# A fused decoder layer on one core: 52 weight blocks multiplied as one 512-column and one 256-column matmul per k-tile, with memory slots of 16 KB

## The chip, the core and the metric

The kernel runs on one core of one Trainium2 chip. The metric is the device time of one execution in microseconds (us). Its engines each run their own instructions in order: TensorE (PE in the profile, its weight loads PEld), VectorE (DVE), ScalarE (ACT), GpSimd (POOL) and SyncE (SP), which here only issues DMAs.

## What is computed

One decoder layer for 256 tokens of 1024 features, in float32: a first layer norm; a token mixer whose two branches (a matrix-memory LSTM of 4 heads, and a gated delta rule with 16 value heads) read one wide input projection; a cross attention into 256 memory tokens; and 32 experts, of which each token takes four. Cut to what matters:

```python
h = layer_norm(x, ln_in_g, ln_in_b)
proj = h @ w_in                                   # q,k,v,o of the LSTM; q,k,v,z of the delta rule; gates
y_ml  = rms(mlstm(q, k, v)) * sigmoid(mo) @ w_branch_ml
y_gdn = rms(delta_rule(conv(q, k, v))) * silu(gz) @ w_branch_gdn
mix = (sigmoid(gate_ml) * y_ml + sigmoid(gate_gdn) * y_gdn) @ w_mix_out
h = layer_norm(ALPHA * h + mix, ...)
h = layer_norm(ALPHA * h + attention(h @ wq, mem @ wk, mem @ wv) @ wo, ...)
out = layer_norm(ALPHA * h + experts(h, top4(softmax(h @ w_router))), ...)
```

All dense products (before the experts) are made to nearly full float32 precision out of a narrower multiply: a number a is held as a high part and a remainder, a = ah + al, and a product is wh·xh + wh·xl + wl·xh.

## The kernel before

**Dense part.** There are 76 blocks of [1024 × 256] weights. `run_blocks` takes them in a fixed order: the keys of the memory (xk, 4 blocks), the convolution's q, k and v (16), the LSTM's q/k (mqk, 4) and v (mv, 4), its gates (gm) and outputs (mo), the product with w_branch_ml (yml, 4), the gates gg (4) and gz (8), the product with w_branch_gdn (br, 8 blocks in pairs that sum into one output), mix (4), then xv (4), xq (4) and wo (4).

A block goes through four steps. SP loads it as two DMAs of 512 KB into one of two `w_raw` buffers (L125); ACT makes the high part in two pieces (L136), DVE the remainder (L137), into four `w_sp` buffers; PE multiplies each half (128 output columns, or 128 tokens where the block "moves", `tm`) over eight k-tiles, with three matmuls of 256 columns per k-tile (L159 to L161, or L154 to L156 for `tm`), 48 in a block. After the first half of the next block, the block's `evac` function reads the result, both halves in one bank of 512 columns of PSUM. `run_blocks` writes all this in one order for every engine; the split of the next block stands ahead of the half that runs.

**Side work.** Generators in `sides` are stepped once after each half: the inverse of the delta rule's triangular matrices (`gen_inv`, L637 and L639, on DVE, beside mqk and mv), the LSTM itself (L839 to L911), and the scan over chunks (L717 to L800, beside gm, mo, yml). No scheduler reorders any of it: what stands first on an engine runs first.

**PSUM** has eight banks: three for blocks (tag `pp`) and five for everything else (tag `pt`).

**Expert part.** 384 tiles of 1 MB stream through a ring of 21 buffers (`load_expert_tile`, L1120 for w_gu, L1124 for w_dn). Seven have a pool of their own (ew1), six lie in the 8 KB slots of `act1` that held dense activations before (ew2), the others in `w_raw`, `w_sp` and the space of a later pool. For each expert eight tiles feed L1636 (64 token slots as weights, 512 moving columns) and four feed L1678. SP issues a load when its buffer is released; a load that waits holds all that follow on SP.

Of the kernel before, what the change touches and what calls it, by code (L numbers as in the profile page):

```python
# [58 lines left out]
class Block:  # L59
    """One [1024, 256] block of weights: its product with 256 columns, and what follows it."""  # L60

    def __init__(self, w2d, r0, c0, x, tm=False, first=True, last=True, evac=None, before=None, after=None):
        self.w2d, self.r0, self.c0, self.x, self.tm = w2d, r0, c0, x, tm
        self.first, self.last, self.evac, self.before, self.after = first, last, evac, before, after
        self.ps, self.half_evac = None, None


@with_exitstack
def tile_layer(ctx: ExitStack, tc: tile.TileContext, A, out, stop=None):
# [14 lines left out]
    act1 = rctx.enter_context(tc.tile_pool(name="act1", bufs=6, side="right"))  # L84
# [3 lines left out]
    act2 = lctx.enter_context(tc.tile_pool(name="act2", bufs=9))  # L88
# [11 lines left out]
    def a2(shape, dt, name):  # L100
        return act2.tile(shape, dt, name=name, tag="a2")

# [13 lines left out]
    def load(b, by_cols=False):  # L116
        b.raw = wpool.tile([128, KT, 256], F32, name="w_raw", tag="w_raw", bufs=2)
        b.hi, b.lo = [], []
# [9 lines left out]
    def split_part(b, c):  # L128
        """the high part (float32r) and what is left: by rows where the block moves, else by columns"""
# [8 lines left out]
        b.hi.append(hi)  # L138
        b.lo.append(lo)

    def half(b, c, ks=None):
        xh, xl = b.x
        if b.ps is None:
            if b.last and not b.half_evac:
# [5 lines left out]
        for k in ks or range(KT):  # L150
            st, sp = b.first and k == 0, b.last and k == KT - 1
            if b.tm:
                wh, wl = b.hi[k // 4][:, k % 4], b.lo[k // 4][:, k % 4]
                nc.tensor.matmul(o, xh[:, k, cs], wh, start=st, stop=False, skip_group_check=True)  # L154
                nc.tensor.matmul(o, xh[:, k, cs], wl, start=False, stop=False, skip_group_check=True)  # L155
                nc.tensor.matmul(o, xl[:, k, cs], wh, start=False, stop=sp, skip_group_check=True)  # L156
            else:
                wh, wl = b.hi[c][:, k], b.lo[c][:, k]
                nc.tensor.matmul(o, wh, xh[:, k], start=st, stop=False, skip_group_check=True)  # L159
                nc.tensor.matmul(o, wh, xl[:, k], start=False, stop=False, skip_group_check=True)  # L160
                nc.tensor.matmul(o, wl, xh[:, k], start=False, stop=sp, skip_group_check=True)  # L161
# [1569 lines left out]
```

## Time and profile before

| | us |
|---|---|
| median of 3 runs | 1552.58 (1550.48 to 1554.14) |
| the profiled execution's own span | 1545.5 |
| PE busy in it | 1449.1 (94%) |
| DVE busy | 572.2 (37%) |
| ACT busy | 396.4 (26%) |
| dense part, to the restart of the weight stream | about 0 to 600 |
| experts | about 600 to 1545 |

The span lies 7.1 us under the median of the runs. Where a later row gives a DMA rate, it is of all the core's traffic in that stretch; a busy share is read stage by stage, since the dense part and the expert part have different limits.

### The profile page before, as it was taken

The page shows a single profiled execution, that of the slowest core. Times are in us where ns is not written, and L with a number is a line of the kernel's source. Part 1 is how long each engine was busy: PE and PEld are TensorE (multiplying, and loading weights), DVE is VectorE, ACT ScalarE, POOL GpSimd, SP SyncE. Part 2 cuts the span into 40 slices and gives each one's busy share as a digit, 9 for nine tenths or more (in the row PEclk, how much of TensorE's full clock was granted, in tenths as well). Part 3 has the DMA queues.
Part 4 walks back from the last instruction along what each step waited for, and adds up shares of the span by engine and source line. Part 5 has one row for each costly group of instructions (what it writes and reads, how often), then busy time and mean ns, then how long its engine had stood idle before and what let it go on. Part 6 is the DMA issues. An engine that isn't in the chain of part 4 may idle for free.

```text
span 1545.5 us, 22348 instructions
## 1 busy us (share of the span) xinstructions
PE 1449.1 (94%) x9411; PEld 871.8 (56%) x9411; DVE 572.2 (37%) x1030; ACT 396.4 (26%) x630; POOL 49.2 (3%) x85
## 2 busy tenths in 40 slices
PE   8899999999999999999999999999999899899894
PEld 7889999999999996333333333333333323323331
DVE  6788875766657564102112111111111111102102
ACT  5766646335534542101101101101001001101101
POOL 3000210000020000000000000000000000000000
PEclk9999999999999999999999999999999999999998
DMA  8444662244676988999999999999999999999995
GB/s 279 137 137 137 192 204 84 83 137 142 197 241 221 336 298 340 410 413 416 417 417 415 416 417 416 414 417 418 415 415 417 417 415 417 416 417 415 416 417 209
DMA packets 158040, 499.85 MB, mean 323 GB/s; under 512 B 9848, under 2 KB 88752, under 8 KB 124400
## 3 DMA queue, kind: packets, MB, share of 16 engines
q1 hardware_dynamic: 154704, 486.57, 80.8%
q0 software_dynamic: 3232, 11.80, 2.3%
q8 instruction: 76, 1.25, 0.3%
q14 instruction: 28, 0.23, 0.0%
HBM read 492.83 MB, written 5.51 MB: 322 GB/s over the span
## 4 chain that ended last, share of the span: by engine, by line
PE 67%; DMA 20%; DVE 7%; ACT 3%; issue 1%; SPq 0%; DVEq 0%; ACTq 0%
PE ps_y L1678 12%; DMA ew<-in_w_gu_dram 10%; PE ps_g L1636 9%; PE ps_u L1636 9%; DMA ew<-in_w_dn_dram 8%; PE ps_proj L159 6%; PE ps_proj L161 6%; PE ps_proj L160 6%; PE ps_xg L1391 4%; PE ps_proj L156 2%; PE ps_proj L154 2%; PE ps_proj L155 2%; PE ps_g L1359 2%; DVE w_sp L137 1%; DMA w_raw<-in_w_branch_gdn_dram 1%
## 5 line engine op out<-in xcount | busy, mean ns | idle before, releaser
L1636 PE MATMUL ps_g<-ew,xg 128*64 128x512 f32 x1024 | 266.7, 599 | 17.4 <-DMA ew<-in_w_gu_dram 17.3
L1495 DVE TENSOR_SCALAR sw_g<-ps_g 128x512 f32<-128x512 f32 x32 | 22.1, 692 | 668.5 <-PE ps_g L1636 668.5
L1636 PE MATMUL ps_u<-ew,xg 128*64 128x512 f32 x1024 | 263.2, 592 | 0.0
L1678 PE MATMUL ps_y<-ew,aT 128*64 128x512 f32 x1024 | 226.8, 595 | 9.2 <-ACT aT L1668 8.6
L137 DVE TENSOR_TENSOR w_sp<-w_raw,w_sp 128x1024 fp32r<-128x1024 f32 x152 | 183.9, 1222 | 97.5 <-ACT w_sp L136 96.8
L159 PE MATMUL ps_proj<-hT_hi,w_sp 128*128 128x256 f32 x640 | 186.1, 291 | 0.0
L160 PE MATMUL ps_proj<-hT_lo,w_sp 128*128 128x256 f32 x640 | 181.6, 284 | 0.0
L161 PE MATMUL ps_proj<-hT_hi,w_sp 128*128 128x256 f32 x640 | 181.5, 284 | 0.0
L136 ACT CAST w_sp<-w_raw 128x1024 fp32r<-128x1024 f32 x152 | 157.3, 1046 | 63.2 <-PE ps_proj L156 18.8
L1636 PEld LDWEIGHTS ps_g<-ew,xg 128*64 128x64 f32 x1024 | 67.1, 136 | 180.6 <-issue 119.4
L1636 PEld LDWEIGHTS ps_u<-ew,xg 128*64 128x64 f32 x1024 | 73.6, 137 | 146.2 <-issue 146.2
L1678 PEld LDWEIGHTS ps_y<-ew,aT 128*64 128x64 f32 x1024 | 70.7, 137 | 144.7 <-issue 126.2
L1497 ACT ACTIVATE sw_s<-sw_g 128x512 f32<-128x512 f32 x32 | 20.1, 629 | 464.2 <-DVE sw_g L1495 464.2
L159 PEld LDWEIGHTS ps_proj<-hT_hi,w_sp 128*128 128x128 f32 x640 | 123.0, 192 | 4.2 <-issue 2.8
L160 PEld LDWEIGHTS ps_proj<-hT_lo,w_sp 128*128 128x128 f32 x640 | 123.2, 192 | 0.0
L161 PEld LDWEIGHTS ps_proj<-hT_hi,w_sp 128*128 128x128 f32 x640 | 123.0, 192 | 0.0
L1681 ACT COPY y<-ps_y 128x512 f32<-128x512 f32 x32 | 18.7, 585 | 231.5 <-PE ps_y L1678 231.5
L1391 PEld LDWEIGHTS ps_xg<-oh,hres 128*128 128x128 f32 x512 | 58.5, 192 | 24.2 <-issue 23.2
L1391 PE MATMUL ps_xg<-oh,hres 128*128 128x128 f32 x512 | 61.5, 278 | 10.5 <-DVE oh L1382 10.4
L1508 PE MATMUL pacc<-y,ct 64*128 64x512 f32 x256 | 63.9, 616 | 0.7 <-ACT y L1681 0.7
L248 ACT ACTIVATE xg<-ps_xg,gbc 128x128 f32<-128x128 f32 x64 | 29.3, 457 | 97.6 <-DVE xg L250 97.6
L250 DVE TENSOR_SCALAR xg<-ps_xg,gbc 128x128 f32<-128x128 f32 x64 | 26.2, 410 | 57.6 <-PE ps_xg L1391 38.3
(443 smaller groups left out, 1853.8 us busy)
## 6 DMA issues: line engine op xcount, KB each, us to landing
ew<-in_w_gu_dram SPq DMA_DIRECT2D x256, 1024.0 KB, 19.9
ew<-in_w_dn_dram SPq DMA_DIRECT2D x127, 1024.0 KB, 20.1
w_raw<-in_w_in_dram SPq DMA_DIRECT2D x88, 512.0 KB, 4.5
w_raw<-in_w_branch_gdn_dram SPq DMA_DIRECT2D x16, 512.0 KB, 4.8
w_raw<-in_xa_wk_dram SPq DMA_DIRECT2D x8, 512.0 KB, 6.9
w_raw<-in_w_branch_ml_dram SPq DMA_DIRECT2D x8, 512.0 KB, 4.1
w_raw<-in_w_mix_out_dram SPq DMA_DIRECT2D x8, 512.0 KB, 4.7
w_raw<-in_xa_wv_dram SPq DMA_DIRECT2D x8, 512.0 KB, 4.5
```

The source lines that it names most:

```text
L136: nc.scalar.copy(hi, raw)
L137: nc.vector.tensor_sub(lo, raw, hi)
L154: nc.tensor.matmul(o, xh[:, k, cs], wh, start=st, stop=False, skip_group_check=True)
L155: nc.tensor.matmul(o, xh[:, k, cs], wl, start=False, stop=False, skip_group_check=True)
L156: nc.tensor.matmul(o, xl[:, k, cs], wh, start=False, stop=sp, skip_group_check=True)
L159: nc.tensor.matmul(o, wh, xh[:, k], start=st, stop=False, skip_group_check=True)
L160: nc.tensor.matmul(o, wh, xl[:, k], start=False, stop=False, skip_group_check=True)
L161: nc.tensor.matmul(o, wl, xh[:, k], start=False, stop=sp, skip_group_check=True)
L1391: nc.tensor.matmul(ps[k // 4][:, k % 4], z[:, t, k * 128:(k + 1) * 128], oh[:, t].rearrange("p e s -> p (e s)"), start=t == 0 and k % 4 == ...
L1508: nc.tensor.matmul(pacc[t][n], ct[q, t * 128:(t + 1) * 128], y[q], start=False, stop=e == NE - 1, skip_group_check=True)
L1636: nc.tensor.matmul(w[n * 64:n * 64 + 64], xg[:, k, ei], wt[e, k][:, c0 + n * 512:c0 + (n + 1) * 512], start=False, stop=k == KT - 1)
L1678: nc.tensor.matmul(py[n * 64:n * 64 + 64], aT[:, k % 4, k // 4], wd[:, n * 512:(n + 1) * 512], start=k == 0, stop=k == KT - 1)
```

## The change

**Wide blocks.** A block marked `wide` makes, per k-tile, one matmul of 512 columns (the high weights against the high and the low columns side by side) and one of 256 (the low weights against the high columns, into the right half of the same bank). The two halves of a bank are then added by `summed`: ACT copies the right 256 columns into SBUF, DVE adds the left ones. The words given with the change say 47 of 76 blocks; in the code 52 are marked: xk, mqk, mv, gm, mo, yml, gz, gg, br, xv and xq. That is 832 matmuls of 512 columns and 832 of 256 in place of 2496 of 256, and 48 outputs with 96 copies and 96 additions. The 24 blocks of the convolution, mix and wo stay.

The results of xk, mv and xv are put by `summed` where they are needed, and their 12 copies of 512 columns (L383, L821, L1188) go. In br, the gate product (L958) takes 512 columns at once, where it took two of 256.

**PSUM.** A wide block needs two banks, so `pp` has four and `pt` four.

**Memory.** High and low parts must lie in one tile, so slots are 16 KB: `act1` has 3 instead of 6 of 8 KB, `act2` 4 and one of 8 KB instead of 9. Two expert tiles of 1 MB then share one `act1` slot, which is released as a whole.

```diff
-        return psum.tile([128, 512], F32, name=name, tag="pp", bufs=3)
+        return psum.tile([128, 512], F32, name=name, tag="pp", bufs=4)
...
-        return psum.tile([128, 512], F32, name=name, tag="pt", bufs=5)
+        return psum.tile([128, 512], F32, name=name, tag="pt", bufs=4)
...
+    def pair(alloc, name):
+        return alloc([128, 2, KT, S], F32R, name)
...
         if b.ps is None:
-            if b.last and not b.half_evac:
+            if b.wide:
+                b.ps = [ps_proj("ps_proj0"), ps_proj("ps_proj1")]
+            elif b.last and not b.half_evac:
...
+                w = b.sp[c][:, :, k]
+                one, two, rest = w[:, 0], xp[:, :, k], (w[:, 1], xp[:, 0, k])
+            if b.wide:
+                nc.tensor.matmul(o, one, two, start=st, stop=False, skip_group_check=True)
+                nc.tensor.matmul(o[:, 256:], *rest, start=False, stop=sp, skip_group_check=True)
+            else:
+                nc.tensor.matmul(o, one, two[:, 0], start=st, stop=False, skip_group_check=True)
+                nc.tensor.matmul(o, one, two[:, 1], start=False, stop=False, skip_group_check=True)
+                nc.tensor.matmul(o, *rest, start=False, stop=sp, skip_group_check=True)
+
+    def summed(b, c):
+        if b.sum is None:
+            b.sum = b.dest() if b.dest else t2([128, 2, 256], "pj_sum")
+        p = b.ps[c]
+        nc.scalar.copy(b.sum[:, c], p[:, 256:])
+        nc.vector.tensor_add(b.sum[:, c], b.sum[:, c], p[:, :256])
...
                 half(b, c)
+                if c == 0 and prev is not None and prev.wide and prev.last:
+                    summed(prev, 1)
+                if c == 1 and b.wide and b.last:
+                    summed(b, 0)
                 step_sides()
                 if c == 0 and prev is not None and prev.last and prev.evac:
-                    spawn(prev.evac(prev.ps))
+                    spawn(prev.evac(prev.sum if prev.wide else prev.ps))
...
         elif r < R1 + 6:
-            w = a1([128, 2 * D], F32, "ew2")
+            if (r - R1) % 2 == 0:
+                W["two"] = a1([128, 2, 2 * D], F32, "ew2")
+            w = W["two"][:, (r - R1) % 2]
```

Two places show where the new instructions stand. The first is DVE in the stretch of mv, where L137 makes remainders of weights and L637 and L639 are the inverse (`inv`). Before:

```order
L137 TENSOR_TENSOR w_sp<-w_raw,w_sp 128x1024 x2
L637 TENSOR_TENSOR inv_1881<-inv_1880 128x11x21
L639 TENSOR_TENSOR inv_1880<-inv_1880,inv_1881 128x11x21
L637 TENSOR_TENSOR inv_1881<-inv_1880 128x10x22
L639 TENSOR_TENSOR inv_1880<-inv_1880,inv_1881 128x10x22
L637 TENSOR_TENSOR inv_1881<-inv_1880 128x9x23
L639 TENSOR_TENSOR inv_1880<-inv_1880,inv_1881 128x9x23
L637 TENSOR_TENSOR inv_1881<-inv_1880 128x8x24
L639 TENSOR_TENSOR inv_1880<-inv_1880,inv_1881 128x8x24
L137 TENSOR_TENSOR w_sp<-w_raw,w_sp 128x1024 x2
```

The same place after the change (L147 is the remainder, L669 and L671 the inverse, L184 the addition in `summed`, `mqkv` the tile that holds the LSTM's values):

```order
L147 TENSOR_TENSOR w_sp<-w_raw,w_sp 128x1024 x2
L184 TENSOR_TENSOR mqkv<-mqkv,ps_proj_2215 128x256
L669 TENSOR_TENSOR inv<-inv 128x11x21
L671 TENSOR_TENSOR inv<-inv 128x11x21
L669 TENSOR_TENSOR inv<-inv 128x10x22
L671 TENSOR_TENSOR inv<-inv 128x10x22
L184 TENSOR_TENSOR mqkv<-mqkv,ps_proj_2270 128x256
L669 TENSOR_TENSOR inv<-inv 128x9x23
L671 TENSOR_TENSOR inv<-inv 128x9x23
L669 TENSOR_TENSOR inv<-inv 128x8x24
L671 TENSOR_TENSOR inv<-inv 128x8x24
L147 TENSOR_TENSOR w_sp<-w_raw,w_sp 128x1024 x2
```

Each block now has two additions between the same remainders and the same eight instructions of the inverse; nothing leaves DVE there.

The second place is ACT in br, where L136 makes high parts of weights and L960 the high part of the merged branches (`mT`). Before:

```order
L136 CAST w_sp<-w_raw 128x1024 x5
L960 CAST mT_hi<-gg 128x512
L136 CAST w_sp<-w_raw 128x1024 x4
L960 CAST mT_hi<-gg 128x512
L136 CAST w_sp<-w_raw 128x1024 x4
```

And after (L146 is the high part of weights, L183 the copy in `summed`, L985 the high part of `mT`):

```order
L146 CAST w_sp<-w_raw 128x1024 x4
L183 COPY pj_sum<-ps_proj_4437 128x256
L146 CAST w_sp<-w_raw 128x1024
L183 COPY pj_sum<-ps_proj_4438 128x256
L985 CAST mT<-hm_gate 128x512
L146 CAST w_sp<-w_raw 128x1024 x3
L183 COPY pj_sum<-ps_proj_4524 128x256
L146 CAST w_sp<-w_raw 128x1024
L183 COPY pj_sum<-ps_proj_4525 128x256
```

Of the four casts of weights between two casts of `mT`, one now stands between two copies that wait for PE.

## Rows read from the trace of the kernel before

**Rows 1.** The page: busy time of each engine, its share of the span, its instructions.

```profile
PE 1449.1 (94%) x9411; PEld 871.8 (56%) x9411; DVE 572.2 (37%) x1030; ACT 396.4 (26%) x630; POOL 49.2 (3%) x85
```

**Rows 2.** Windows: stretch, its length, busy time of each engine, granted clock, DMA share, GB/s.

```profile
core 0: us, PE busy (x) PEld busy (x) DVE busy (x) ACT busy (x) POOL busy (x), PEclk, DMA share, GB/s
176.00:216.00 40.00, 40.00 (x336) 40.00 (x335) 37.61 (x76) 20.43 (x30) 0.00 (x0) 1.00 0.58 185
216.00:352.00 136.00, 135.30 (x1469) 123.96 (x1467) 87.17 (x133) 58.59 (x94) 8.43 (x13) 1.00 0.36 113
352.00:428.00 76.00, 75.40 (x632) 75.43 (x633) 50.52 (x55) 43.21 (x56) 2.05 (x4) 1.00 0.58 184
428.00:476.00 48.00, 46.34 (x383) 45.13 (x381) 27.28 (x33) 18.31 (x21) 6.77 (x15) 1.00 0.67 214
496.00:560.00 64.00, 63.93 (x492) 62.16 (x492) 38.95 (x52) 33.91 (x55) 1.62 (x3) 1.00 0.91 328
660.00:1520.00 860.00, 798.17 (x3946) 291.96 (x3942) 135.38 (x292) 77.02 (x145) 0.00 (x0) 1.00 1.02 416
```

**Rows 3.** Timeline of PE: start, duration, line, tiles, weights, moving columns.

```profile
239.88 0.28 PE L159 MATMUL ps_proj<-hT_hi,w_sp 128*128 128x256 f32 x1
240.00 0.28 PE L160 MATMUL ps_proj<-hT_lo,w_sp 128*128 128x256 f32 x1
```

**Rows 4.** Timeline of PE: small matmuls, eight in the first row.

```profile
66.50 1.06 PE L479 MATMUL ps_gtot<-r,stack 16*128 16x16 f32 x8
67.42 0.20 PE L483 MATMUL ps_gtot<-ident,row_tmp 4*128 4x4 f32 x1
```

**Rows 5.** Timeline of PE among the experts: three rows of four lie between.

```profile
892.22 1.03 PE L1636 MATMUL ps_g<-ew,xg 128*64 128x512 f32 x4
...
895.65 0.60 PE L1636 MATMUL ps_g<-ew,xg 128*64 128x512 f32 x2
```

**Rows 6.** Groups by line and form: busy time, mean ns, idle before.

```profile
L958 DVE TENSOR_TENSOR gg<-gg,ps_proj 128x256 f32<-128x256 f32 x8 | 3.1, 416 | 0.4 <-PE ps_proj L161 0.4
L862 ACT ACTIVATE hm<-ps_mn,ml_v 128x256 f32<-128x256 f32 x8 | 3.4, 471 | 1.8 <-DVE ml_v L860 1.8
L383 ACT COPY kT_sp<-ps_proj 128x512 f32<-128x512 f32 x4 | 2.3, 580 | 0.0
```

**Rows 7.** Timelines of DVE and of PE beside mv.

```profile
206.94 0.36 DVE L639 TENSOR_TENSOR inv<-inv,inv 128x192 f32<-128x192 f32 x1
207.22 2.35 DVE L137 TENSOR_TENSOR w_sp<-w_raw,w_sp 128x1024 fp32r<-128x1024 f32 x2
210.74 0.28 PE L155 MATMUL ps_proj<-w_sp,hT_hi 128*128 128x256 f32 x1
```

**Rows 8.** Timelines of DVE and PE in the scan.

```profile
282.90 0.69 DVE L721 TENSOR_TENSOR vP<-vP,sc_t 128x512 f32<-128x512 f32 x1
283.98 1.09 PE L729 MATMUL ps_vn<-vP,x_t 64*64 64x128 f32 x16
```

**Rows 9.** Br: ACT's casts as a group, then timelines of ACT and PE.

```profile
L136 ACT CAST w_sp<-w_raw 128x1024 fp32r<-128x1024 f32 x17 | 17.0, 1047 | 18.1 <-DMA w_raw<-in_w_branch_gdn_dram 17.3 <-PE ps_proj L161 0.9
425.40 0.60 ACT L931 ACTIVATE gate_s<-ps_proj 128x512 f32<-128x512 f32 x1 [3.71 <-PE ps_proj L161]
475.95 0.39 PE L156 MATMUL ps_proj<-w_sp,mT_lo 128*128 128x256 f32 x1 [0.23 <-DVE mT_lo L961]
```

**Rows 10.** Waits of PE in the first 70 us: total, times, longest.

```profile
PE ps_gcol L456 <- DVE stack L447: 3.0, 1, 3.0
```

**Rows 11.** SP's issues in the first expert; second and last row: median us to landing.

```profile
613.28 4.12 SPq L1120 DMA_DIRECT2D ew<-in_w_gu_dram  x2
ew<-in_w_gu_dram SPq DMA_DIRECT2D x1, 1024.0 KB, 10.5
622.17 2.04 SPq L1120 DMA_DIRECT2D ew<-in_w_gu_dram  x2
w_raw<-in_w_in_dram SPq DMA_DIRECT2D x88, 512.0 KB, 4.5
```

More of the change, by code (lines that the diff above doesn't have):

```diff
@@ L59, with __init__ @@
 class Block:
-    def __init__(self, w2d, r0, c0, x, tm=False, first=True, last=True, evac=None, before=None, after=None):
+    def __init__(self, w2d, r0, c0, x, tm=False, first=True, last=True, evac=None, before=None, after=None, wide=False,
+                 dest=None):
         self.w2d, self.r0, self.c0, self.x, self.tm = w2d, r0, c0, x, tm
@@ L65, in __init__ @@
         self.ps, self.half_evac = None, None
+        self.wide, self.dest, self.sum = wide, dest, None
 @with_exitstack
@@ L152, in half @@
             if b.tm:
[L153 to L156, printed above, removed]
-            else:
[L158 to L161, printed above, removed]
+                w = b.sp[k // 4][:, :, k % 4]
+                one, two, rest = xp[:, 0, k, cs], w, (xp[:, 1, k, cs], w[:, 0])
+            else:
+                w = b.sp[c][:, :, k]
[13 more added lines that the diff above has]
+        nc.vector.tensor_add(b.sum[:, c], b.sum[:, c], p[:, :256])
     def step_sides():
@@ L215, in run_blocks @@
             prev = b
+        if prev is not None and prev.wide and prev.last:
+            summed(prev, 1)
         if prev is not None and prev.evac:
-            spawn(prev.evac(prev.ps))
+            spawn(prev.evac(prev.sum if prev.wide else prev.ps))
     def evac_now(gen):
@@ L376, in gen_ln_in @@
             yield
-        for i, _ in enumerate(transpose_split(hres, hT_hi, hT_lo, gbc)):
+        for i, _ in enumerate(transpose_split(hres, hT, gbc)):
             if i % LK == LK - 1:
@@ L684, in f @@
             if not vP:
-                for i in range(2):
-                    vP.append(a2([128, 4, NCH, 128], F32, f"vP{i}"))
+                vP_ = a2([128, 2, 4, NCH, 128], F32, "vP")
+                vP.extend(vP_[:, i] for i in range(2))
             y = conv_taps(ps, 16 + 2 * u)
@@ L791, in gen_scan @@
         nc.vector.reciprocal(t, t)
-        oT = C["oT"] = [a2([128, KT, S], F32, f"oT{g}") for g in range(2)]
+        oT_ = a2([128, 2, KT, S], F32, "oT")
+        oT = C["oT"] = [oT_[:, g] for g in range(2)]
         for g in range(2):
@@ L991, in ev_norm @@
         return f
-    xh = (hT_hi, hT_lo)
+    xh = hT
     wbm, wbg = A["w_branch_ml"][0], A["w_branch_gdn"][0]
-    seq = [Block(A["xa_wk"][0], 0, u * 256, (memT_hi, memT_lo), evac=ev_xk(u)) for u in range(4)]
+    seq = [Block(A["xa_wk"][0], 0, u * 256, memT, evac=ev_xk(u), wide=True,
+                 dest=lambda u=u: kT_sp[:, 2 * u:2 * u + 2]) for u in range(4)]
     conv = []
@@ L1150, in affine2, with vk @@
         affine_col(dst, src, gbc[:, 16 + k:17 + k], gbc[:, 24 + k:25 + k], on_act)
+    def vk():
+        if "vk" not in XA:
+            XA["vk"] = a1([128, 2, 2 * D], F32, "xvk")
+        return XA["vk"]
     def gen_ln1():
```

192 lines of the change are left out of this document (92 added, 100 removed).

## The prediction, made before the changed kernel was run

> **What bounds the kernel now.** The first view is the page's list of busy engines [rows 1]: PE 94% of the span, and no other engine above 56%. That share is a mean over two regimes, so the second view is the windows [rows 2]. From 660 to 1520 us the DMA share is 1.02 at 416 GB/s: there the weight stream sets the time, and fewer PE instructions buy nothing. In the dense windows the DMA share is 0.36 to 0.67 up to 476 us, and PE is busy 40.00 of 40.00, 135.30 of 136, 75.40 of 76, 46.34 of 48: PE sets the time, except that DVE is nearly as full in the first of them (37.61 of 40) and that PE has holes in the last. The stream restarts from an empty queue at about 600 us, so what the dense part gains or loses moves the end by as much. The granted clock is 1.00, its higher level, in all these windows.
>
> **Price of a k-step.** In the window of 40.00 us PE made 336 matmuls of 256 columns: 119.0 ns each [rows 2], as the timeline shows one by one [rows 3]; a k-step of three costs 357 ns. Is this the columns or the loading of 128 columns of weights? Eight small matmuls with 128 weight columns but only 16 moving columns go from 66.50 to 67.42, 115 ns each [rows 4]: weights alone take nearly the whole pace. A matmul of 512 columns is seen among the experts: 16 from 892.22 to 895.65, 214.4 ns each [rows 5], with 64 weight columns. In a wide block the 512 columns should cover the loading, and the 256 columns after them stay at 119: 214.4 + 119.0 = 333.4 ns, 23.7 saved. Bounds: if the small one shrank to half of 214.4, the saving is 357 − 321.6 = 35 ns; if the 119.0 − 107.2 = 11.8 ns above the columns' share were a fixed cost of each matmul, one such is saved, 11.8 ns. I take 23.7, since the small matmuls point at the weights. A block has 16 k-steps, 0.38 us; 52 blocks 19.7 us, between 9.8 and 29.
>
> The Trainium skill, "TensorE: Matmul & The Clock Gate", section "Back-to-back issue gap", puts an isolated matmul at N/2.4 + 2.5 ns, 109 ns for 256 columns and 216 for 512; three would be 328 and the wide step 325, and the change would save 2 us in all. The trace disagrees on the first figure (119.0) and agrees on the second (214.4). Section "LDWEIGHTS" of that page puts the load of 128 columns at 107 ns by their number, near the 115 here; it lies on the side of the reading that I chose.
>
> **What is added.** Each of 48 outputs costs two copies on ACT and two additions on DVE. The nearest rows are a DVE product of 128x256 from PSUM, 416 ns, and an ACT instruction of 128x256 from PSUM, 471 ns; each copy of 580 ns that goes was one of 12 [rows 6]. So DVE gets 96 × 0.416 = 40 us, ACT 96 × 0.471 − 12 × 0.58 = 38 us. They cost nothing where these engines have room and PE does not wait behind them. Stretch by stage:
>
> *Front (xk, 4 blocks, −1.5 at best).* PE later waits 3.0 us for DVE's rows [rows 10]; what PE gains before runs into that wait, and additions in the same queue push it. I take +0.3, ends −1.5 and +1.0.
>
> *mqk, mv (8 blocks, −3.0 at best).* DVE runs here without a gap: the inverse's instruction of 206.94 ends where the remainders of 207.22 begin. Their first is needed at 210.74, and was done 2.35/2 after 207.22, at 208.4: 2.3 us of slack [rows 7]. The 16 additions are 6.7 us; the window's idle time takes 2.4 of them, that slack 2.3, and 2.0 would be left. But the inverse's instructions get shorter at its end, and the first gm block has more slack. I take 0: all of the 3.0 is lost; ends −1.5 and +4.3 (6.7 − 2.4).
>
> *gm, mo, yml (12 blocks, −4.5 at best).* DVE is busy 87.2 of 136 us and gets 10 more. But the scan runs through DVE: L721 ends at 283.59 and its matmuls start at 283.98 [rows 8], a margin of 0.39, less than one addition. I charge four such places, 4 × 0.42 = 1.7, and take −2.8; ends −4.5 and −0.5.
>
> *gg, gz (12 blocks, −4.5 at best).* DVE has 50.5 of 76, ACT 43.2, and they get 10 and 11: 60 and 54 of some 71. I take off 0.8 for the two additions and copies that can stand before a split: −3.7; ends −4.5 and −2.0.
>
> *br and the start of mix (8 blocks, −3.0 at best).* ACT waits 17.3 us here for weights to land [rows 9]: load, cast, remainder, PE. A faster PE waits longer, so none of the 3.0 is taken. Ahead of br the last gz output passes one more copy and one more addition (0.9) before ACT's L931 at 425.40, and the casts for br stand behind it on ACT. At the end the matmul that waited for DVE at 475.95 [rows 9] gets the copy and addition too, less what one product of 512 columns saves against two: +0.7. For the copies between the casts I add 0.4. Sum +2.0; ends −3.0 and +4.0.
>
> *xv, xq (8 blocks, −3.0 at best).* PE 63.93 of 64, DVE 39, ACT 34 [rows 2]; the attention's chain at its end gets one copy and one addition, and an earlier stretch of it another. −1.8; ends −3.0 and 0.
>
> *PSUM.* One bank fewer for side work: I take 0, since what they hold is read by one instruction of about half a microsecond [rows 6]; where a matmul lacked its bank it would wait for one such.
>
> Dense sum: 0.3 + 0 − 2.8 − 3.7 + 2.0 − 1.8 = −6.0 us.
>
> **Expert tiles in pairs.** A slot of two tiles is released when both were read. SP issues a tile at 613.28, which before waited for L1636 alone; its partner is issued at 622.17, when the first w_dn tile was read by L1678 [rows 11]. After the change both wait for that, and all that stands behind on SP with them. The tile of 613.28 landed 10.5 us later, at 623.8; at 2.5 us for a megabyte (416 GB/s, [rows 2]) the one before it landed at 621.3, and nothing is in flight then. A tile into an empty queue takes about as long as a 512 KB load of the dense part, 4.5 us [rows 11]: 622.2 + 4.5 = 626.7, 2.9 late. A lost DMA interval in this part is lost for good, unless the stream has other dips to fill. Take +2.6; ends +0.9 and +3.2. Later pairs lie deeper in the ring, with more in flight.
>
> **Sum.** −6.0 + 2.6 = −3.4 us: span 1545.5 − 3.4 = 1542.1. The span lies 7.1 under the median, so the median comes to 1549.2 us.
>
> **The rivals.**
>
> (a) *The secondary engines have room.* The margins give way nowhere but in br: −19.7 + 3.0 = −16.7 and a bubble of 0.9: −15.8, 1536.8 us; with half of the difference to the forecast, 1543. For it: DVE and ACT are busy under 70% outside mqk and mv. Against it: orders are fixed, and slack here is a few tenths to 2 us.
>
> (b) *DVE becomes the bound in mqk and mv, slower than before.* If the slack there is used up by the third block, the stretch costs +4.3, the inverse and all of the scan behind it start later (−0.5 in place of −2.8), and br takes its +4.0: −3.4 + 4.3 + 2.3 + 2.0 = +5.2, 1557.8 us; with the worst of all stages 1561. It decides from 3.4 us of added DVE delay on. For it: DVE at 94% there. Against: PE needs less time only if it is fed, so both ends can't be reached at once.
>
> (c) *The 512 columns cost as much as two of 256* (238 ns in place of 214.4): nothing is saved. Then scan, gg, gz, xv, xq cost 1.7 + 0.8 + 1.2 where they gained, m about +2, front and br as above, and the bubble stays: 0.3 + 2 + 3.7 + 2.0 + 2.6 = +10.6, 1563 us. Against it: [rows 5]. The rule of the first section cited would end close to this, at 1561.
>
> (d) *The experts don't notice the pairs*, or the queue drains twice: 2.6 us either way, part of the forecast's own spread.
>
> **How the numbers follow.** A measurement of this kernel tells about 0.2%, 3.1 us, from no change: faster is below 1549.5, slower above 1555.7. The forecast (a gain of which two thirds is eaten, 1545 to 1554) has 0.46, half of it on either side of 1549.5; its own range is 1545 to 1554. (a) has 0.24; (b) 0.24, of it 0.03 within 0.2%; (c) 0.06. Faster: 0.23 + 0.24 = 0.47, less 0.01 for the near end of (a): 0.46. Same: 0.23 + 0.03 = 0.26. Slower: 0.21 + 0.06 = 0.27, with that 0.01 0.28. The range leaves out the far half of (a) and the far end of (b) with (c): 1540 to 1560.
>
> **What would show it.** Wide matmuls in the timeline should start 214 and 119 ns apart by turns; 226 and 119 means a fixed cost, 238 means (c). In the window of mqk and mv DVE should have no gap and PE waits for remainders that were not there before; with no such waits (a) is on its way. In br ACT's wait for weights should stay near 17 us and PE's holes grow. At the first expert SP should hold one tile until the first w_dn tile is read, and the DMA share should drop there for some 3 us. The forecast is wrong if the dense part, up to the first expert's matmuls, ends more than 10 us earlier, or later than before.

## The result, and the profile after

The changed kernel takes 1560.89 us in the median (1558.62 to 1565.29), against 1552.58 before: 1.0065 times as long, with a 95% interval of 1.0048 to 1.0083. It is slower where a small gain was forecast, and 0.9 us above the range of 1540 to 1560. The time lies between rival (b)'s 1557.8 and its worst of 1561; its mechanism is only one part of it.

The profiled execution has a span of 1556.9 us; the same execution was timed at 1558.62, 1.7 us more. The page's first part:

```profile
PE 1449.9 (93%) x8579; PEld 827.7 (53%) x8579; DVE 602.5 (39%) x1122; ACT 418.5 (27%) x714; POOL 48.1 (3%) x83
```

PE is busy as long as before [rows 1] with 832 matmuls fewer. This line alone doesn't say why; by the pace measured below, 832 k-steps save 5.5 us in all, 0.4% of the busy time. The windows of the same stretches as in [rows 2], with the same columns:

```profile
176.00:216.00 40.00, 38.88 (x219) 33.06 (x218) 38.14 (x81) 22.24 (x39) 0.00 (x0) 1.00 0.58 177
216.00:352.00 136.00, 134.10 (x1277) 112.30 (x1276) 97.14 (x164) 63.19 (x114) 7.32 (x11) 1.00 0.35 108
352.00:428.00 76.00, 74.66 (x436) 64.96 (x435) 58.72 (x81) 50.86 (x82) 1.64 (x3) 1.00 0.60 184
428.00:476.00 48.00, 44.04 (x240) 37.57 (x239) 28.52 (x34) 20.27 (x28) 7.77 (x16) 0.96 0.64 210
496.00:560.00 64.00, 60.82 (x354) 52.53 (x352) 43.26 (x72) 34.57 (x62) 0.00 (x0) 1.00 0.77 271
660.00:1520.00 860.00, 798.96 (x3950) 291.72 (x3948) 132.66 (x289) 76.94 (x144) 0.00 (x0) 1.00 1.02 416
```

In the first, DVE now has 38.14 of 40 us and PE, full before, 38.88. PE stands idle for longer than before in every dense stretch, most in the last two (44.04 of 48, 60.82 of 64). The expert stretch (the last line) is the same: 416 GB/s, DMA share 1.02.

A k-step of a wide block, timeline of PE at the same place as [rows 3]:

```profile
239.17 0.40 PE L171 MATMUL ps_proj<-hT,w_sp 128*128 128x512 f32 x1
239.40 0.28 PE L172 MATMUL ps_proj<-hT,w_sp 128*128 128x256 f32 x1
239.52 0.40 PE L171 MATMUL ps_proj<-hT,w_sp 128*128 128x512 f32 x1
239.76 0.28 PE L172 MATMUL ps_proj<-hT,w_sp 128*128 128x256 f32 x1
```

The 512 columns take 0.23 to 0.24 us, the 256 after them 0.12. In gz, where both kernels run without a break, the starts of the k-steps lie 353 ns apart in the mean and 360 before; in br 347 and 352. That is the first surprise: 5 to 7 ns saved, not 23.7. Of the paces that the prediction listed as signs, this is nearest to (c).

From the timelines of PE, the stages' lengths against the first profile of before (in us; the last column is a second profile of the kernel before, to be told of below). Each stage is counted by the starts of its matmuls. One border lies otherwise than its name says: br's first matmul starts at 425.20, and the 430.8 used here, and in the expectations as "the first matmul of br", is the start of br's second block.

| stage, from and to in the first profile of before | forecast | changed | before again |
|---|---|---|---|
| front, to 89.4 | +0.3 | −0.4 | +1.5 |
| mqk, mv, 169.4 to 217.8 | 0 | +1.0 | 0.0 |
| gm, mo, yml, 217.8 to 353.0 | −2.8 | +0.6 | +1.5 |
| gg, gz and the first block of br, 353.0 to 430.8 | −3.7 | −1.2 | 0.0 |
| the other seven blocks of br and the first of mix, 430.8 to 479.4 | +2.0 | +4.4 | +1.5 |
| the rest of mix, xv, xq, 479.4 to 556.6 | −1.8 | +3.4 | 0.0 |
| wo, to the 21st expert tile's landing at 604.2 | 0 | +0.4 | +0.1 |
| from there to the end | +2.6 | +3.2 | +0.1 |
| sum | −3.4 | +11.4 | +4.7 |

Against the second profile of before the changed kernel loses 6.7 us, against the first 11.4; the timed medians lie 8.3 apart.

### The profile page after: what moved, and what is told of

Read it like the earlier page. It is cut to its first block, busy times and chain, and to the rows that moved or that the text cites. A ratio compares the mean times of both kernels' runs of the same rounds, so it can differ in the third digit from the quotient of the medians.

```text
span 1556.9 us, 20832 instructions
## 1 busy us (share of the span) xinstructions
PE 1449.9 (93%) x8579; PEld 827.7 (53%) x8579; DVE 602.5 (39%) x1122; ACT 418.5 (27%) x714; POOL 48.1 (3%) x83
## 3 DMA queue, kind: packets, MB, share of 16 engines
q8 instruction: 70, 1.15, 0.3%
## 4 chain that ended last, share of the span: by engine, by line
PE 50%; DMA 27%; DVE 13%; ACT 5%; issue 3%; SPq 0%; DVEq 0%; ACTq 0%
DMA ew<-in_w_gu_dram 13%; DMA ew<-in_w_dn_dram 10%; PE ps_y L1707 10%; PE ps_g L1665 8%; PE ps_u L1665 8%; PE ps_proj L171 4%; DVE w_sp L147 4%; PE ps_xg L1420 3%; PE ps_proj L172 2%; ACT w_sp L146 2%; PE ps_proj L174 2%; PE ps_proj L176 2%; PE ps_proj L175 2%; DMA w_raw<-in_w_in_dram 2%; PE ps_g L1388 1%
## 5 line engine op out<-in xcount | busy, mean ns | idle before, releaser
L147 DVE TENSOR_TENSOR w_sp<-w_raw,w_sp 128x1024 fp32r<-128x1024 f32 x152 | 184.0, 1223 | 92.9 <-ACT w_sp L146 92.4
L146 ACT CAST w_sp<-w_raw 128x1024 fp32r<-128x1024 f32 x152 | 157.1, 1046 | 46.7 <-DMA w_raw<-in_w_branch_gdn_dram 17.2
L171 PE MATMUL ps_proj<-hT,w_sp 128*128 128x512 f32 x384 | 138.3, 402 | 0.0
L172 PE MATMUL ps_proj<-hT,w_sp 128*128 128x256 f32 x384 | 107.7, 280 | 0.1
L171 PEld LDWEIGHTS ps_proj<-hT,w_sp 128*128 128x128 f32 x384 | 72.1, 188 | 16.7 <-issue 0.5
L174 PE MATMUL ps_proj<-hT,w_sp 128*128 128x256 f32 x256 | 75.5, 295 | 0.0
L176 PE MATMUL ps_proj<-hT,w_sp 128*128 128x256 f32 x256 | 73.5, 287 | 0.2 <-DVE w_sp L147 0.2
L175 PE MATMUL ps_proj<-hT,w_sp 128*128 128x256 f32 x256 | 73.3, 286 | 0.0
L172 PEld LDWEIGHTS ps_proj<-hT,w_sp 128*128 128x128 f32 x384 | 72.6, 189 | 0.4 <-DVE w_sp L147 0.4
```

The source lines that it names most:

```text
L146: nc.scalar.copy(hi, raw)
L147: nc.vector.tensor_sub(lo, raw, hi)
L171: nc.tensor.matmul(o, one, two, start=st, stop=False, skip_group_check=True)
L172: nc.tensor.matmul(o[:, 256:], *rest, start=False, stop=sp, skip_group_check=True)
L174: nc.tensor.matmul(o, one, two[:, 0], start=st, stop=False, skip_group_check=True)
L175: nc.tensor.matmul(o, one, two[:, 1], start=False, stop=False, skip_group_check=True)
```

## Experiments

**The pace of matmuls alone.** Twelve stretches of 96 matmuls (in two of them 192, by turns of 512 and 256 columns) on weights and columns that lie still (N is 12; `xp` holds its two halves in two pieces, `xs` in one; `wb` and `xb` are bfloat16, the others float32r, the 4-byte type of the dense part's products, which the timeline prints as f32). The lines shown are L46, L48 and L49, then L54, L62, L64, L66 and L68:

```diff
+    for i in range(8 * N):
+        mm(pb[:, :256], w[:, i % 8], xp[:, i % 2, i % 8], **f)
+    for i in range(8 * N):
+        mm(pa, w[:, i % 8], xp[:, :, i % 8], **f)
+        mm(pb[:, :256], w[:, (i + 3) % 8], xp[:, 0, i % 8], **f)
...
+        mm(pa, w[:, i % 8], xs[:, i % 8], **f)
...
+        mm(pc, w[:, i % 8, :64], xs[:, i % 8], **f)
...
+        mm(pd[:, :256], w[:, i % 8, :32], xs[:, i % 8, :256], **f)
...
+        mm(pa[:, :256], wb[:, i % 8], xb[:, i % 8, :256], **f)
...
+        mm(pb, wb[:, i % 8], xb[:, i % 8], **f)
```

> A kernel of matmuls alone, in twelve stretches of 96 (two of them of 192), with nothing else running; it computes nothing of the layer. Theory COLUMNS (the pace of these matmuls is set by their moving columns, about 0.456 ns each, so that the weights were hidden all along): 256 columns take 116 to 119 ns with 128, 64 or 32 weight columns alike; 512 columns take 230 to 234 ns, alone or by turns with 256. Theory WEIGHTS (the prediction's: 119 ns is the load of 128 weight columns, and columns cost 0.417 ns): 512 columns 214 to 216 ns, 256 columns with 64 or 32 weight columns 107 to 109 ns. Theory STRIDE (the two halves of the 512 columns lie 8 KB apart, and the jump costs): 512 columns in one piece 214 to 216 ns, in two pieces 230 or more. With 128 and with 64 moving columns and 128 weight columns all theories expect the weights' own pace to show, about 107 to 115 ns.

Groups by line, with busy time and mean duration of one (busy time by 96 is the pace within some 2 ns, as the last one's length is in it):

```profile
L46 PE MATMUL pb<-xp,w 128*128 128x256 f32 x96 | 11.7, 283 | 0.0
L54 PE MATMUL pa<-xs,w 128*128 128x512 f32 x96 | 21.9, 389 | 0.0
L62 PE MATMUL pc<-xs,w 128*64 128x512 f32 x96 | 22.2, 392 | 0.0
L64 PE MATMUL pd<-xs,w 128*32 128x256 f32 x96 | 11.1, 276 | 0.0
L66 PE MATMUL pa<-xb,wb 128*128 128x256 bf16 x96 | 10.7, 273 | 0.0
L68 PE MATMUL pb<-xb,wb 128*128 128x512 bf16 x96 | 20.9, 379 | 0.0
```

From start to start, 256 columns take 120.0 ns with 128 weight columns and 113.4 with 32; 512 columns alone 226.9 with 128, 229.9 with 64. The timeline by turns:

```profile
60.08 0.28 PE L49 MATMUL pb<-xp,w 128*128 128x256 f32 x1
60.19 0.40 PE L48 MATMUL pa<-xp,w 128*128 128x512 f32 x1
60.43 0.28 PE L49 MATMUL pb<-xp,w 128*128 128x256 f32 x1
60.54 0.40 PE L48 MATMUL pa<-xp,w 128*128 128x512 f32 x1
```

By turns 512 and 256 columns take 236.7 and 116.7 ns in the mean of 96, and the same (236.7 and 116.7) where the 512 lie in one piece: 353.4 against 3 × 120 = 360, 6.6 ns saved. Theory STRIDE falls. WEIGHTS falls for the 512 columns (227, not 214) and for 256 with 32 weight columns (113, not 107 to 109). COLUMNS is the nearest, though its ranges are missed too: these columns cost 0.44 ns each (227 / 512, 113 / 256), and with 128 weight columns 256 of them take 6.6 ns more. By turns the pair takes 13 ns more than its 768 columns (353.4 against 340.3), so that dropping one matmul of three drops a third of some 20 ns. In bfloat16 the same shapes take 109 and 216 ns. With 128 weight columns and only 128 moving ones the pace is 111 ns, the weights' own, as all theories expected; with 64 moving ones it is 112 at first and then 213 to 215, since the granted clock fell there:

```profile
137.50:141.50 4.00, 4.00 (x39) 1.00 0.00 0
144.00:148.00 4.00, 4.00 (x21) 0.50 0.00 0
```

**Memory without wide blocks.** All blocks with three matmuls of 256, in the changed memory:

```diff
+WIDE = ()
...
-    gm_b = [Block(w_in, 0, GM0 + u * 256, xh, evac=ev_gm(u), wide=True) for u in range(4)]
+    gm_b = [Block(w_in, 0, GM0 + u * 256, xh, evac=ev_gm(u), wide="gm" in WIDE) for u in range(4)]
...
```

> The changed kernel with no wide block: memory in slots of 16 KB, four banks for blocks and four for the rest, tiles in pairs, but three matmuls of 256 columns per k-tile and no additions. Theory SPLIT (the dense part's loss comes from the additions and copies, the memory costs only in the experts): the dense part as before, the expert stream's 21st tile issued within 1 us of the 599.5 us of before, the 28th landing 3.4 us later than it, the median 3 us above the kernel before, about 1555.5. Rival MEMORY (fewer slots and banks hold up dense work too): the 21st tile issued 3 us or more later than before, the median 6 us or more above.

Median 1554.56 against 1551.31 on that chip; ratio 1.0012, interval 0.9995 to 1.0029. Windows of PE in gg and gz, and in the hole of the stream, where SP stands from 617.4 to 627.7 us:

```profile
358.00:436.00 78.00, 78.00 (x656) 1.00 0.66 207
620.00:630.00 10.00, 9.54 (x57) 1.00 0.61 242
```

In this profile mqk to mv, gg to gz, br, mix and xv are as before to 0.02 us, xq is +0.3, and from the 21st tile's landing to the last one's it is +3.9 (+2.9 to the end of the span). The front is 3.7 later, since the last load of xk landed 5 us late, and the scan 1.5, since PE ran at its lower clock near 250 us. By these two shifts the 21st tile was issued 5.5 us later than before, which was MEMORY's sign; but the kernel before shows shifts of both kinds (below), the front of the changed kernel, with the same memory, none (−0.4), and the median is 3.2 higher, as SPLIT said. So SPLIT holds: memory and banks cost the dense part nothing that was seen, and the pairs cost the stream.

**The kernel before once more.**

```diff
 (the kernel before, unchanged)
```

> The kernel before once more, for how much one profiled execution of the same program differs from another. Up to the 10th half block (44 us) the changed memory's runs differ by up to 3.7 us among themselves, by a load of xk that lands late. Theory NOISE: this profile too starts its convolution up to 1.5 us away from the first one's, and its span is 1 to 5 us over 1545.5, since the time of the runs is 1.7 us over their span and the median of before is 1552.6. Rival: the first profile is reproduced within 0.3 us, so that these differences belong to the changed memory.

Windows of PE, with granted clock, DMA share and GB/s:

```profile
44.00:60.00 16.00, 14.14 (x108) 0.85 0.54 170
246.00:252.00 6.00, 6.00 (x69) 0.72 0.01 3
428.00:476.00 48.00, 45.64 (x375) 1.00 0.63 200
```

This profile has a span of 1550.2 us (timed 1551.97, 1.8 more), 4.7 above the first: 1.5 in the front, where the last load of xk landed 2.7 us later, 1.5 by a stretch at a clock of 0.72 near 250 us, where the first profile had 1.00, and 1.5 in br. NOISE holds: the first profile was a short execution of that kernel. Of the 7.1 us that the prediction added to its span, 1.7 are what every timed run has over its span; the rest is how short that one execution was.

**The ring's order.** One entry of the order moved, so that both tiles of every pair are asked for one after the other:

```diff
-        r = n if n < RING - 1 else (list(range(8)) + [RING - 1] + list(range(8, RING - 1)))[(n - RING + 1) % RING]
+        r = n if n < RING - 1 else (list(range(7)) + [RING - 1] + list(range(7, RING - 1)))[(n - RING + 1) % RING]
```

> The changed kernel with one entry of the order of the ring moved: after the first round the single tile of the last pool comes before the pair whose two tiles were the last of w_gu and the first of w_dn, so that no pair is asked for with another tile in between. Theory HOLE (SP stands at the first tile of that pair from 620 to 630 us, the queue drains and the stream loses 3.3 us for good): the dense part unchanged, the last tile lands 2.5 to 3.3 us earlier than in the changed kernel, the median 1557.5 to 1558.5. Rival: the single tile's buffer or the pair comes free no earlier, the hole moves by a tile: gain below 1 us.

SP and the DMAs in the changed kernel: the last issue ahead of the wait, the one after it, and the window between them (DMA share and GB/s at the end):

```profile
619.78 0.33 SPq L1148 DMA_DIRECT2D ew<-in_w_gu_dram  x1
630.38 0.33 SPq L1148 DMA_DIRECT2D ew<-in_w_gu_dram  x1
620.00:630.00 10.00, 9.54 (x62) 1.00 0.76 315
```

And with the order moved:

```profile
621.80 2.04 SPq L1161 DMA_DIRECT2D ew<-in_w_gu_dram  x2
620.00:630.00 10.00, 10.00 (x62) 1.00 1.02 423
```

In the changed kernel SP stands from 620.1 to 630.4, and the window moves 315 GB/s. Moved, SP's waits there are some 5 us, and the window moves 423 GB/s. From the 21st tile's landing to the last one's the loss falls from 3.2 to 0.6 us (to the end of the span, from 3.2 to 1.0); HOLE holds. The median is 1558.39 (1.0047, 1.0032 to 1.0062, against 1.0065 of the changed kernel). Its dense part, to the 21st tile's landing, is 12.1 us over the first profile's, 3.9 more than the changed kernel's; 2.1 of that is in xq, where PE had a clock of 0.76 from 536 to 543 us, 1.5 in the front and 0.7 in gm to yml. So the price of the dense part differs from one execution to the next.

**The memory keys' input later.**

```diff
     def load_mem2():
         XA["m"] = pair(a1, "memT2")
+        nc.gpsimd.tensor_copy(gate1, mT[0][0:1, 1, 4, 0:1])
         nc.gpsimd.dma_start(XA["m"].rearrange("p a k t -> p (a k t)"), memT_d)
```

> The changed kernel with the 2 MB of memory keys' input, which POOL fetches at the start of br, held back until the third of four outputs of br is done. Theory COLLISION (in br the casts come later than before, so that the next load of weights is issued beside those 2 MB, PE starves for over 3 us and its clock drops): PE's waits for w_sp in br fall from 4 us to under 1, the half-speed stretch at 442 to 446 us goes, the start of mix comes 3 us earlier, the median 1557.5 to 1558.5. Rival CHAIN (the copies and additions alone make br late, whatever the other loads do): br ends within 1 us of the changed kernel. Rival LATE (what waits behind on POOL, or the memory's transfer itself, is late for the cross attention): br gains, and xv or xq gives it back.

First the changed kernel in br: SP's load of br's third block, POOL's load of 2 MB, ACT's casts on either side of the wait for that block, PE's first hole, and PE's window after it (clock third from the end):

```profile
426.31 0.92 SPq L135 DMA_DIRECT2D w_raw<-in_w_branch_gdn_dram  x2
425.71 0.53 POOL L1102 DMA_DIRECT2D memT<-memT_d  x1 [71.73 <-PE ps_proj L172]
429.50 2.00 ACT L146 CAST w_sp<-w_raw 128x1024 fp32r<-128x1024 f32 x2
438.15 1.99 ACT L146 CAST w_sp<-w_raw 128x1024 fp32r<-128x1024 f32 x2 [6.66 <-DMA w_raw<-in_w_branch_gdn_dram]
439.25 0.51 PE L171 MATMUL ps_proj<-og,w_sp 128*128 128x512 f32 x1 [1.79 <-ACT w_sp L146]
442.00:446.00 4.00, 4.00 (x15) 0.60 0.76 254
```

The third block is issued at 426.31 (in the kernel before at 422.46, ahead of POOL's at 425.54), 0.6 us behind the 2 MB. Its second half lands at 438.05, 11.7 us later (5.0 in the kernel before), and its cast starts at 438.15. PE stands, and in the window from 442 to 446 its granted clock is 0.60. With the 2 MB held back, windows of PE in br and in mix with the start of xv:

```profile
428.00:476.00 48.00, 45.28 (x258) 1.00 0.59 197
476.00:500.00 24.00, 21.39 (x158) 0.93 0.94 297
```

Br, from its second block on, takes 41.8 us (42.35 before, 45.6 changed), and the stretch at the lower clock is gone there. So COLLISION holds for br, though PE's waits for w_sp in it fall only to 1.5 us, not under 1. But mix and xv give all of it back: from the first matmul of mix to the first of xq it takes 6.4 us more than before, where the changed kernel takes 1.0 more. LATE holds too: the median, 1562.42 (1.0070, 1.0047 to 1.0093), is no lower than the changed kernel's.

**The last two gz blocks as before.**

```diff
-    gz = [Block(w_in, 0, GZ0 + u * 256, xh, evac=ev_gz(u), wide=True) for u in range(8)]
+    gz = [Block(w_in, 0, GZ0 + u * 256, xh, evac=ev_gz(u), wide="gz" in WIDE and u < 6) for u in range(8)]
```

> The changed kernel with the last two of the eight gz blocks as before, the rest wide, br too. From the first matmul of br to the first of mix the kernel before takes 42.35 us, the changed one 45.6 us. Theory COLLISION (the copies and additions of the last gz blocks delay the casts for br, and by them the load of br's third block, which then runs beside the 2 MB from POOL): the third load is issued 3 us earlier than in the changed kernel, near 423 us, and br takes 42 to 43.5 us. Rival BR (br's own copies and additions do it): 45 us or more.

ACT's casts and PE's window:

```profile
427.62 2.94 ACT L147 CAST w_sp<-w_raw 128x1024 fp32r<-128x1024 f32 x3
431.35 1.05 ACT L147 CAST w_sp<-w_raw 128x1024 fp32r<-128x1024 f32 x1 [0.78 <-PE ps_proj L173]
428.00:476.00 48.00, 45.35 (x262) 1.00 0.68 218
```

The load of br's third block begins to be issued at 424.3, 2.0 us earlier (3 were expected) and ahead of the 2 MB at 426.0, three casts run in a row at 427.62 and the fourth at 431.35, and br takes 42.5 us. The five kernels that have wide blocks on both sides of that border, and the 2 MB in their place, take 45.1 to 45.8; the others 41.8 to 43.8. So br's 3.3 us came from the two blocks ahead of it, not from its own copies and additions, which cost 0.2 net of what PE saves. The first block of mix stays 1.15 longer, as in every run with br wide (2.4 where the 2 MB came late), and not in those without. Timed once: 1554.85.

**mqk and mv as before.**

```diff
-    side_m = ([Block(w_in, 0, MQ0 + u * 256, xh, evac=ev_mqk(u), wide=True) for u in range(4)] +
+    side_m = ([Block(w_in, 0, MQ0 + u * 256, xh, evac=ev_mqk(u), wide="mqk" in WIDE) for u in range(4)] +
...
```

> The changed kernel with the eight blocks of mqk and mv as before (three matmuls of 256 columns, no additions), the rest wide. From the first matmul of mqk to the first of gm the kernel before takes 48.4 us, the changed one 49.35 us. Theory DVE (16 additions in a DVE that has no room push the remainders onto the moment of their use): 48.4 us within 0.2, remainders of mv ready 1.9 us or more before use. Rival BANKS (four banks of PSUM and the other slots hold PE up there): over 49 us.

The changed kernel in mv, timelines of DVE and PE:

```profile
203.92 2.35 DVE L147 TENSOR_TENSOR w_sp<-w_raw,w_sp 128x1024 fp32r<-128x1024 f32 x2
206.19 0.42 DVE L184 TENSOR_TENSOR mqkv<-mqkv,ps_proj 128x256 f32<-128x256 f32 x1
205.19 0.50 PE L171 MATMUL ps_proj<-w_sp,hT 128*128 128x512 f32 x1 [0.49 <-DVE w_sp L147]
```

The first of two remainders ends near 205.1 and PE, which waited 0.49 us for it, starts at 205.19; before there were 2.3 us between such a pair [rows 7]. With mqk and mv as before the stretch takes 48.40 us again, where the changed kernel takes 49.35, and PE no longer waits there: DVE holds. There is more to it: in four of the six runs with mqk and mv wide, PE waits 1.0 to 1.3 us for DVE's vP in the scan, near 285 us, and loses that time; in the other two it had already lost 1.5 us at the lower clock before that place. In the two runs with mqk and mv as before and some blocks wide there is no such wait; but in one of them, this one, PE had lost time at the lower clock too, so that only one is left as a witness. Timed once: 1559.39.

**xq as before.**

```diff
-    xq_b = [Block(A["xa_wq"][0], 0, u * 256, None, wide=True) for u in range(4)]
+    xq_b = [Block(A["xa_wq"][0], 0, u * 256, None, wide="xq" in WIDE) for u in range(4)]
```

> The changed kernel with the four xq blocks as before, the rest wide. From the first matmul of xq to the first of wo the kernel before takes 40.6 us, the changed one 44.1 us. Theory ATTENTION (each head's scores wait for a copy, an addition and a scaling of its queries, and copies that wait for PE stand before casts of weights on ACT): 40.6 to 41.2 us, the median 3 us under the changed kernel's. Rival WEIGHTS (the expert tiles that SP issues there, and the loads behind them, come in another order since their slots come free at other times): 43 us or more.

Waits of PE from 515 us, in total, times, longest, in the changed kernel (its three lines), and its first line in the run with the last two gz blocks as before:

```profile
PE ps_xs L1231 <- ACT x_q L1259: 1.7, 1, 1.7
PE ps_proj L172 <- DVE w_sp L147: 0.8, 2, 0.5
PE ps_proj L171 <- DVE h1T L298: 0.6, 1, 0.6
PE ps_xs L1244 <- ACT x_q L1272: 0.8, 2, 0.5
```

And with xq as before:

```profile
PE ps_proj L177 <- DVE w_sp L148: 0.9, 2, 0.5
PE ps_proj L176 <- DVE h1T L307: 0.3, 1, 0.3
```

The scores (ps_xs) no longer wait for scaled queries (x_q), and the stage takes 42.2 us in place of 44.1. With xq wide it loses 1.3 to 5.6 us in six runs, and 0.8 to 2.7 of that is this wait, in each of the six; with xq as before and xv wide it loses 0.7 and 1.7 in two runs, and no run with xq as before has the wait. So the wait that ATTENTION names is shown, with its price. That it is the whole is not: neither theory's range is met, and the waits for w_sp and for the normalised rows (h1T) stay with xq as before. WEIGHTS, another order of the loads, isn't tested for this rest. The median, 1562.31 (1.0079, 1.0060 to 1.0098), isn't lower than the changed kernel's: the 2 us are within what executions differ by.

**What is added, without what is saved.**

```diff
-                nc.tensor.matmul(o, one, two, start=st, stop=False, skip_group_check=True)
+                nc.tensor.matmul(o[:, :256], one, two[:, 0], start=st, stop=False, skip_group_check=True)
+                nc.tensor.matmul(o[:, 256:], one, two[:, 1], start=st, stop=False, skip_group_check=True)
```

> The changed kernel with each matmul of 512 columns made as two of 256 into the two halves of the same bank: all that the change adds (copies, additions, memory, pairs) without what it saves on PE. From the first matmul of gg to the first of br the kernel before takes 77.85 us, the changed one 76.6 us. Theory PACE (a k-step of 512 and 256 columns is only 7 ns shorter than three of 256, and additions cost nothing where DVE has room): 77.7 to 78.0 us there. Rival HIDDEN GAIN (the wide k-step saves the 23.7 ns of the prediction, and additions eat two thirds of it even there): 80 us or more. From the first matmul of mqk to the first of gm (48.4 before, 49.35 changed): 49.3 to 50 us by both, since DVE sets the time there.

Here the second matmul opens its half of the bank by itself, which leaves out part of the wide blocks' sums; no instruction of the dense part is chosen by a value, and only that part's times are read. PE in gg and gz (with br's first block), in this run and, below it, in the kernel before:

```profile
358.00:436.00 78.00, 78.00 (x655) 1.00 0.61 194
353.00:431.00 78.00, 78.00 (x657) 1.00 0.61 195
```

655 matmuls in 78.00 us are 119.1 ns each: PE has no gap, and the stretch takes 77.85 us as before, against 76.6 with 512 columns. PACE holds: additions are free there, and the wide k-step saves 1.2 us in 208 (13 blocks), 5.9 ns each. In mqk and mv this run takes 49.3.

**Wide only where there is room.** xk, gm, mo, yml, gg, six of gz and xv wide (30 blocks), and the ring's order moved:

```diff
+WIDE = ('xk', 'gm', 'mo', 'yml', 'gz', 'gg', 'xv')
...
-    gg = [Block(w_in, 0, GG0 + u * 256, xh, evac=ev_gg(u), wide=True) for u in range(4)]
+    gg = [Block(w_in, 0, GG0 + u * 256, xh, evac=ev_gg(u), wide="gg" in WIDE) for u in range(4)]
```

> Wide blocks only where DVE and ACT have room and no chain waits for them: xk, gm, mo, yml, gg, the first six gz, and xv (30 blocks); mqk, mv, br, xq and the last two gz as before; the order of the ring as in the run that removed the hole. By 7 ns saved for each of 480 k-steps PE saves 3.4 us; the scan takes back about 1, the ring 0.3. Theory SUM (the loss of the changed kernel is the sum of the places named, and the gain per k-step is 7 ns): 1 to 3 us under the kernel before, ratio 0.998 to 0.9995. Rival (something else in memory or banks costs): 1 us or more above the kernel before.

1553.04 against 1550.59: ratio 1.0017, 1.0005 to 1.0029. SUM falls in its total: the gains are there (−0.25 in gm to yml, −1.1 in gg and gz, −0.5 in xv), 1.8 us in all and not 2.4, but xq is 0.7 longer, br 1.3 (as in the second profile of the kernel before), and from the 21st tile's landing to the last one's the stream still loses 2.2 us, where the same order of the ring had left 0.6. The rival's sign, 1 us or more above the kernel before, is met (2.5), and of what memory and banks could cost, only the stream shows a loss. What the stream's rest is made of wasn't tried. No choice of wide blocks that was run beats the kernel before.

**The kernel before with half of the memory keys' input later.**

```diff
         for i in range(2):
             XA["m"] = XA.get("m", ()) + (a1([128, KT, S], F32R, f"memT2_{i}"),)
+            if i:
+                nc.gpsimd.tensor_copy(gate1, mT[1][0:1, 2, 0:1])
             nc.gpsimd.dma_start(XA["m"][i].rearrange("p k t -> p (k t)"), memT_d[i])
```

> The kernel before with the second of the two 1 MB loads of the memory keys' input held back on POOL until the second of br's four outputs is done, the first left where it is. Theory COLLISION (these loads and the parameters behind them hold up br's weights in the kernel before too, whose PE has 2.3 us of holes there): from the first matmul of br to the first of xv 66.1 us before, 64.5 here; median 1 to 1.5 us under the kernel before, ratio 0.999. Rival LATE (the second half then meets the loads of mix, as when all of it was held back): 66 us or more, ratio 1.000 or above.

From br's second block to xv it takes 67.1 us, median 1550.69, ratio 1.0003 (0.9991 to 1.0016): the first six blocks of br gain 2 us, and the last two lose 3 when the second half arrives. COLLISION's gain doesn't come and LATE's sign is met; as a total, 67.1 lies between the two profiles of the kernel before (66.1 and 67.6). The place where POOL's 2 MB cost nothing wasn't found.

## Why the prediction was wrong

**The price of a k-step** is the step that failed, and alone it turns the sign. It took 214.4 ns for 512 columns from the expert's matmuls [rows 5]. Those are no single stream, as a closer look at the kernel before shows (two rows of its timeline):

```profile
891.79 0.60 PE L1636 MATMUL ps_u<-ew,xg 128*64 128x512 f32 x2
892.22 0.60 PE L1636 MATMUL ps_g<-ew,xg 128*64 128x512 f32 x2
```

Each row is two matmuls of 64 weight columns that start 7 ns apart and write to the two halves of one bank's partitions; the next two start 0.43 us later. The 214 ns were the mean of two that take twice as long together. Their operands are plain float32 besides (`xg` and `ew` in the kernel), where the blocks multiply float32r; the timeline prints f32 for both. The small matmuls that made the prediction choose the weights' side were no better a guide: the weights' own pace is 111 ns in the run of matmuls alone, under the 120 that 256 columns take. The prediction's lower bound (11.8 ns saved) was still too high; the measured 6.6 lies outside its two ends, and rival (c), a k-step with no saving, was nearly right and had 0.06. Put 6.6 in its place (0.106 us for a block), and the forecast's own sum is: gm to yml −1.3 + 1.7, gg and gz −1.3 + 0.8, xv and xq −0.8 + 1.2, with 0.3, 2.0 and 2.6 as they were and mqk and mv at the 0 that it took: +5.2 us, near 1558; with +2.0 − 0.8 for mqk and mv (what the working left over, less the gain) +6.4, near 1559. Both are slower than before, and both lie inside the range; that the time fell beyond it came from what br, xv and xq cost besides. By the table the sum is off by 14.8 us: 8.6 to 9.8 of them are this price, 2.4 br, some 3 xv and xq with the price put right. That the median is off by 11.7 only is due to the first profile, which was short.

**The rule set aside.** That of "Back-to-back issue gap" in the Trainium skill's "TensorE: Matmul & The Clock Gate" was nearer with its small saving (2.5 ns against 6.6 measured), by figures of which this type of data reaches neither: 120 and 227 ns against 109 and 216. With bfloat16 the run shows these figures. The prediction set it aside because its first figure didn't match, and kept a row that was of another kind of work. That its estimate of 1561 by this rule is the measured 1560.9 is luck for the most part: it left out some 5 us of what br, xv and xq cost, and against that it counted from a short profile, which the changed kernel exceeds by 3 us more than the medians differ.

**What is added** was sized well or too high: in the changed kernel the addition takes 415 ns (416 assumed) and the copy 368 (471 assumed). In the whole DVE is busy for 30 us more (40 assumed) and ACT for 22 (38 assumed):

```profile
L184 DVE TENSOR_TENSOR pj_sum<-pj_sum,ps_proj 128x256 f32<-128x256 f32 x72 | 29.9, 415 | 1.8 <-ACT pj_sum L183 1.7
L183 ACT COPY pj_sum<-ps_proj 128x256 f32<-128x256 f32 x72 | 26.4, 368 | 2.3 <-PE ps_proj L172 2.3
```

**mqk and mv**: DVE as the bound is right, the slack used up as rival (b) said; +1.0, within the ends. PE's wait of 1 us in the scan behind it was in (b), not in the forecast. **Front**: −0.4, within the ends; executions of the kernel before differ there by 1.5. **PSUM** at 0 is borne out by the run without wide blocks.

**gm to yml and gg, gz**: the losses charged to margins (1.7 and 0.8) were about right or too high; the gains, −4.5 each at best, were 1.3.

**br**: the sum (+2.0) named the longer way from the last gz block to the casts, but not what stands at its end: a load that comes 3.9 us later falls behind 2 MB of another queue and lands 11.7 us after its issue; PE stands, and its granted clock falls soon after. +4.4 (1.15 of it in the first block of mix), just over the upper end of 4.0.

**xv and xq**: the one place where the sign of a stage was wrong for a reason of its own. The prediction counted one copy and one addition in the attention's chain as a loss on a gain. PE waits twice for scaled queries there, 2.0 us in all in this profile and 0.8 to 2.7 in the six with xq wide. That casts wait behind copies on ACT for the rest is argued, not shown. +3.4 by the table; xq alone 3.5, and 1.3 to 5.6 in the six.

**The pairs**: right in mechanism, place and size (+2.6 forecast, 3.2 measured, its upper end), and for the most part undone by one entry of the ring's order (0.6 left in one run, 2.2 in another).

**The offset** of 7.1 us between span and median was 1.7 of the kernel's and the rest one execution's. The prediction's own sign of being wrong, a dense part that ends later than before, came: 8.2 us later by the 21st tile's landing.

Still open: what the 6.6 ns of a matmul with 128 weight columns are, the rest of xq's loss, and why the stream loses 2 us after the 21st tile in the run with 30 wide blocks.

## What to carry to other kernels

Before a duration is taken from another line, look at one instruction of it by itself: type (as the kernel declares it), operand widths and what runs beside it must be those of the new instruction, and a stretch of such matmuls alone costs one run. Ask of work that is moved to engines with spare time not how busy they are, but what stands behind it in their order, down to the load that is issued when they are done. And profile the kernel before twice, since one execution can be several microseconds short in places that a change is then blamed for.

## What the runs showed of the hardware

Matmuls in float32r take 0.44 ns per column (227 ns for 512) at a granted clock of 1.00, those in bfloat16 0.42 (216), and with 128 columns of weights a matmul of 256 in float32r takes 120 ns where 32 columns of weights leave 113. Two plain float32 matmuls of 64 weight columns that write to the two halves of the partitions ran side by side (7 ns apart, the next two 423 ns later); matmuls of 64 weight columns that write to the same half ran one after another (230 ns apart for 512 columns in float32r). The clock fell to its lower level not only in long waits. In br, after holes of 1.8 and 0.75 us, its mean from 442 to 446 us was 0.60. Near 250 us some executions show 0.72 over 6 us with no wait in PE, just after 2.1 us of 64 small matmuls of 32 × 32, and others of the same program 1.00. And among the matmuls alone it was 0.50 from 144 to 148 us, with PE full, in the stretch of 64 moving columns.
